# Two one-column VectorE operations of the softmaxes, with their further columns as per-partition scalars

## The chip, the cores and the metric

The kernel runs on one core of one Trainium2 chip. The metric is the time of one execution on the device, in microseconds (us). The core has a matrix engine (TensorE, PE in the rows; its weight loads are shown apart as PEld), three engines for elementwise work (VectorE or DVE, ScalarE or ACT, GpSimd or POOL), and SyncE (SP), which here only issues DMA transfers. Each engine takes its instructions in the order in which the program has them; semaphores hold an instruction until those it depends on are done.

## The reference

One decoder layer on 1024 tokens of 1024 features, in float32, in this order:

- a projection of the normalised input; its columns feed two groups of attention heads
- eight differential heads: `a = softmax(q1 k1 + bias) - lam * softmax(q2 k2 + bias)`, then `a @ v`, where `bias` falls with the distance of the positions and a causal mask is laid over both maps
- eight latent heads: `softmax(q k) @ v` with the causal mask
- the normalised heads through an output projection, added to the input
- attention to 256 memory tokens, and a mixture of 32 experts of which each token takes two; a last normalisation

The change lies in the two kinds of softmax over the 1024 tokens.

## The kernel before

All functions record instructions in a list; a planner (class `Sched`) with a small cost model starts them one after the other on a model of the engines, and the order in which it starts them is the order in the program. Its inputs are the recorded order, the dependences between the tiles, the room in the tile pools, and costs in nanoseconds: for VectorE `cost` (lines 232 to 238) charges 68 + 1.045 per element, with 60 more where an operand called `scalar` or standing third in an operation named `scalar...` is a tile, and 65 + 0.53 per element for a `tensor_scalar` in SBUF, with 60 more if any operand behind the first input is a tile. Nearly all instructions pass through one line, L481, so rows of the profile are told apart by the names of tiles.

The attention goes over items of one head and one half of the queries (512 of them, four blocks of 128). An item's softmaxes (`s_unit`) are recorded between the products with the values of the item before (`t_unit`, `f_unit`); other work (the memory's keys and values, parts of the output projection) is spread among them by a table of due times.

For a block of 128 queries, with one query per partition, the latent softmax (`softmax_mla`, L1020) multiplies queries and keys on TensorE into one or two banks of 512 keys, takes each bank's negated maximum on VectorE (`tensor_reduce`, L1032) into a column of the small tile `mx`, takes the smaller of the two columns where there are two banks (L1037, in 32 blocks: four of each of the eight heads), and lets ScalarE compute the exponentials with that column as bias and their sums (L1039). The bank comes free for TensorE after that.

The differential softmax (`softmax_diff`, L993) has two maps. For each, one VectorE instruction per bank adds the distance bias to the scores and keeps the minimum in a column of `mx` (L1006; CUSTOM_DVE_ANT_0 in the rows), and ScalarE makes the exponentials and their sums (L1011). Then VectorE takes the reciprocal of the second sum (L1013) and multiplies it with two further columns, `neglam` (minus lambda) and the first sum (L1014, in 64 blocks); with the product as a scalar per row GpSimd multiplies the second map and adds it to the first (L1015 and 1016; with FLEX = 4 the way on VectorE is not offered). These GpSimd operations read and write up to 1024 columns in SBUF. `mx` has seven buffers.

GpSimd also adds the two halves of a head's output (`O<-O,sh`), and makes some of the differences of split weights (`wlo`) and of `mix`. Further small chains on VectorE, `rs`, `g` and `fs`, are the norms' reciprocal roots, on 1 to 32 columns.

Of the kernel before, what the change touches and what calls it, by code (L numbers as in the profile page):

```python
# [17 lines left out]
OP = mybir.AluOpType  # L18
# [61 lines left out]
# Instructions are recorded with the tiles they read and write, and issued in the order in which  # L80
# a list scheduler with a simple cost model starts them.
# [6 lines left out]
def _sizes(side, kw, shape=None):  # L88
    """The axes of one side of a rearrange pattern, as lists of names."""
    out, group = [], None  # L90
    for tok in side.replace("(", " ( ").replace(")", " ) ").split():
        if tok == "(":
            group = []
        elif tok == ")":
            out.append(group)
            group = None
        elif group is None:
            out.append([tok])
        else:
            group.append(tok)  # L100
    return out


class View:
    """A part of a lazily allocated tile."""
# [58 lines left out]
class LazyTile:  # L164
    def __init__(self, pool, shape, dtype, kw, slot):
        self.pool, self.shape, self.dtype, self.kw, self.slot = pool, tuple(shape), dtype, kw, slot
        self.real, self.log, self.left, self.end = None, [], 0, 0
        self.seq, self.strict, self.reserve = slot["count"], False, slot["reserve"]
        self.cap = pool.sched.caps.get(kw["name"])
        slot["count"] += 1  # L170
        # a PSUM bank is taken only once all that is to be written there by the tensor engine can be
        self.whole, self.wait, self.at = pool.psum and kw["name"] != "acc", 0, 0
# [29 lines left out]
class Sched:  # L202
    def __init__(self, nc):
        self.nc, self.ops = nc, []
        self.free = dict.fromkeys(("tensor", "vector", "scalar", "gpsimd", "sync"), 0)
        self.dma_free, self.table = 0, 0
        # for tiles of some names, the places that they share
        self.caps = {n: [0] * c for n, c in dict(CAPS, bank=NB_S, acc=NB_A, lbank=NB_L).items()}
        self.window, self.busy, self.warm = 0, 0, False
        for e in self.free:  # L210
            setattr(self, e, Engine(self, e))
# [7 lines left out]
    def cost(eng, name, a, k, out, views):  # L219
        """Nanoseconds on the engine, and until the result is there."""  # L220
# [27 lines left out]
    def either(self, *ways):  # L248
        """Records an instruction, or a few of one engine; several ways: the scheduler chooses one."""
# [22 lines left out]
        for v in views:  # L272
# [3 lines left out]
            # the tensor engine's writes to a bank stay in order  # L276
# [3 lines left out]
            for o, b, ow in t.log:  # L280
                # the engines take turns at a bank, whatever they do there
                if o is not op and (t.pool.psum and (o.eng != eng or eng is None) or (w or ow) and (
                        fill and o.eng == "tensor" or all(x[0] < y[1] and y[0] < x[1] for x, y in zip(b, box)))):
                    op.deps.add(o)
# [8 lines left out]
    @staticmethod  # L293
    def hold(*views):
        """Instructions recorded after the next flush use these tiles too."""
        for v in views:
            v.tile.left += 1
# [6 lines left out]
    def flush(self):  # L304
# [17 lines left out]
        queue = {e: [] for e in self.free}     # (time ready, idx, op)  # L322
        avail = {e: [] for e in self.free}     # (idx, op)
# [6 lines left out]
        while done < len(ops):  # L330
            best = None
            for e in self.free:
# [4 lines left out]
                # the first one whose tiles have room  # L337
# [54 lines left out]
    @staticmethod  # L392
    def seen(op, eng):
        """When an engine can go on from an instruction."""
        if "dma" in op.name:
            return op.end
        if op.eng == eng == "tensor":
            return op.start
        return op.end + LAT[op.eng].get(eng, 170)

    def room(self, op):
        """When the tiles that the instruction is the first to use can be had; None: not known yet."""
# [16 lines left out]
        for slot, n, before, reserve in need.values():  # L419
            # some places are for the tiles that come before in program order  # L420
# [38 lines left out]
    def clock(self, now, cost):  # L459
        """The tensor engine's clock is halved after a window in which it was little busy."""  # L460
# [55 lines left out]
def hybrid_kernel(ctx: ExitStack, tc: tile.TileContext, a, out):  # L516
# [28 lines left out]
    # everything of size is a tile of 4 KB per partition  # L545
# [8 lines left out]
    def carve(name):  # L554
        """Small tensors as parts of such a tile."""
# [77 lines left out]
    def rsqrt(dst, v, tmp):  # L633
        """dst = 1 / sqrt(v): a first guess from the bits, and three steps of Newton's."""
# [7 lines left out]
    def rsqrt_mean(dst, ss, n, tmp):  # L642
        """dst = 1 / sqrt(ss / n + eps); ss is lost."""
# [3 lines left out]
    def two(name):  # L647
        """Two parts of a [128, 512] operand."""
        return t4(name, P, 2, CH, dt=F32R)
# [13 lines left out]
    def split(dst, src, g=None, eng="vector"):  # L663
        """src (times g) as the sum of two parts that the tensor engine takes exactly."""
# [7 lines left out]
    class Weights:  # L672
        """Column blocks of weights, loaded ahead of their use, in parts [rows, 128 of them, columns]."""
# [16 lines left out]
        def get(self, i):  # L690
            """A function from the row block to its two parts."""
# [12 lines left out]
    def weave(*lists):  # L704
        """Calls the units of all lists, each list's spread evenly over all or a part of the time."""
# [8 lines left out]
    # =================== projections ===================  # L714
# [26 lines left out]
    def x_first(t):  # L741
        """The same for one tile, so that the first products need not wait for a chunk."""
# [20 lines left out]
    # low-rank queries, keys and the rotary key, token-major  # L763
# [22 lines left out]
    # angles of the rotary part  # L786
# [4 lines left out]
    def reduce_angle(ang, tmp):  # L791
        """ang modulo 2 pi, within [-pi, pi] but for rounding"""
# [10 lines left out]
    def c_angles():  # L803
# [6 lines left out]
        # feature-major tables: even heads' has the rotary rows last, odd heads' first; the other rows scale only  # L810
# [32 lines left out]
    def out_split(po, dsts, g=None):  # L843
        """Two parts of a PSUM bank, stored; dsts: where to, and from which partitions."""
# [5 lines left out]
    # rotary key, four copies side by side  # L850
# [25 lines left out]
    # differential queries and keys  # L876
# [15 lines left out]
    # latent queries: columns of a head as [no position | rotary | rotary, halves swapped],  # L892
    # odd heads with the first part last
# [39 lines left out]
    def v_out(po, n0, nh, dst, t):  # L933
        """Values of nh heads from n0 on as [high | low] (even heads) and [low | high]."""
# [36 lines left out]
    # =================== attention ===================  # L971
# [12 lines left out]
    def make_dist(i):  # L984
        """-|pos_q - pos_k| / scale, and far below zero above the diagonal"""
# [7 lines left out]
    def softmax_diff(h, i, q, k, pt):  # L993
# [20 lines left out]
        nc.vector.scalar_tensor_tensor(mx[:, 4:5], mx[:, 3:4], neglam, sums[:, i, h:h + 1], op0=OP.mult, op1=OP.mult)  # L1014
# [5 lines left out]
    def softmax_mla(h, i, q, k, pt):  # L1020
# [14 lines left out]
        if len(scs) > 1:  # L1035
            top = mx[:, 2:3]
            nc.vector.tensor_tensor(top, mx[:, 0:1], mx[:, 1:2], op=OP.min)  # L1037
# [29 lines left out]
    def item(kind, h, c):  # L1067
        """Units of one head and half of its queries: the softmaxes, the products with the values."""
# [73 lines left out]
    def attention(items):  # L1142
        """All units of some items: an item's softmaxes along with the products of the one before."""
# [7 lines left out]
    # =================== output projection, memory, router ===================  # L1151
# [8 lines left out]
    # memory's keys and values  # L1160
# [47 lines left out]
    # output norms: one factor for each token and head  # L1208
# [70 lines left out]
    def factors(c, tiles, name):  # L1279
        """1 / rms of the rows of some tiles, in two steps."""  # L1280
# [10 lines left out]
    def cross_units(c):  # L1291
        """The rows of a chunk, transposed, times the gain and in two parts; their factors are for later."""
# [12 lines left out]
    # cross-attention  # L1305
# [78 lines left out]
    # router  # L1384
# [26 lines left out]
    def r_T(t, kk):  # L1411
        """Half a tile's columns, transposed and in two parts."""
# [19 lines left out]
    def r_keep(t):  # L1432
        """The tile's normalised rows, kept in DRAM for the experts."""
# [6 lines left out]
    def r_factors(c, *sizes):  # L1440
        """Units of the rows' factors, and of the tiles' transposes, logits and rows."""
# [16 lines left out]
    def first_max(v, m, oh, cm, wcol):  # L1458
        """One-hot of the first largest along the last axis, and the largest, step by step."""
# [16 lines left out]
    def r_top(c):  # L1476
        """The chunk's choices of experts."""
# [20 lines left out]
    def r_weights(c, take, gl, gm, goh, m12):  # L1498
# [15 lines left out]
        # in three exact parts  # L1514
# [13 lines left out]
    def r_rank(c):  # L1528
        """Rank of each choice among its expert's."""
# [25 lines left out]
    def r_index():  # L1555
        """The table of the first NS choices of every expert."""
# [15 lines left out]
    def r_slots():  # L1572
        """The weights of the table's choices."""
# [15 lines left out]
    def r_over():  # L1589
        """Blocks beyond an expert's first: how many, and where they start."""  # L1590
# [17 lines left out]
    # =================== experts ===================  # L1608
# [12 lines left out]
    def moe_piece(e, j):  # L1621
        """Of an expert's six pieces: two row blocks of gate and up each, or a row block of down."""
# [21 lines left out]
    def m_x(e):  # L1644
        """Gathers the expert's tokens and transposes them."""
# [81 lines left out]
    # =================== the order of it all ===================  # L1727
# [21 lines left out]
    # units of work on a common time line, which gives the priorities  # L1749
# [9 lines left out]
    def place(units, *knots):  # L1759
        """Spreads units over the stretches between knots, as many on each."""  # L1760
# [57 lines left out]
    # choices beyond an expert's first NS, in blocks of one expert each  # L1818
# [10 lines left out]
    with tc.If(rnov > 0):  # L1829
# [30 lines left out]
        # a choice that is among the first NS matches no lane  # L1860
# [88 lines left out]
    # =================== end: sum and norm ===================  # L1949
# [40 lines left out]
```

## Time and profile before

| | |
|---|---|
| runs | median 1263.01 us of 3 (1262.37 to 1264.27) |
| profiled execution | span 1263.7 us; no other time is given for it, so the span is taken as its own time |
| busy, share of the span | PE 89%, PEld 72%, DVE 72%, ACT 64%, POOL 33% |
| granted TensorE clock, mean | 0.928 |
| chain of waits | PE 49%, DMA 24%, DVE 15%, ACT 6% |

A busy share is the mean over stages. The first 180 us are projections, from 180 to 610 us the attention with other work in between, to 780 us the output projection and the memory attention, and from there to the end the router and the experts. The chain of waits is the work that ended last, followed from the last instruction back to what released it at each step.

### The profile page before, as it was taken

How to read it: one execution, taken by the hardware profiler on the slowest of the kernel's cores; microseconds unless marked ns; L12 is line 12 of the kernel's file. 1: busy time of each engine (PE TensorE's matmuls, PEld its weight loads, DVE VectorE, ACT ScalarE, POOL GpSimd, SP SyncE). 2: the span in 40 equal slices, each digit the busy share in tenths (PEclk: the TensorE clock that was granted, in tenths of full speed). 3: DMA queues.
4: the chain of work that ended last, by engine and by line, in shares of the span. 5: the costliest groups of instructions: out<-in, count | busy, mean ns of one | idle time of the engine just before them, and what ended most of it. 6: DMA issues, size and time to landing. Idle time of an engine off the chain costs nothing.

```text
span 1263.7 us, 19612 instructions
## 1 busy us (share of the span) xinstructions
PE 1119.0 (89%) x6285; PEld 915.9 (72%) x6285; DVE 903.8 (72%) x2100; ACT 803.1 (64%) x1597; POOL 423.3 (33%) x370
## 2 busy tenths in 40 slices
PE   4999999998888998888999999995999988888970
PEld 3988888896767876677899888874666656566640
DVE  5846525478799889988573467786678877777855
ACT  5744326679786778777371455632677877777862
POOL 2214311278554555746411001233133322221110
PEclk8999999997898999788999999995999999999995
DMA  9039897359636462445531132766899999999977
GB/s 291 18 106 314 316 356 223 110 169 265 155 96 146 123 162 62 114 121 194 173 122 47 34 103 70 284 233 232 251 293 275 299 291 311 307 316 315 334 218 272
DMA packets 177883, 256.56 MB, mean 203 GB/s; under 512 B 17035, under 2 KB 131058, under 8 KB 177778
## 3 DMA queue, kind: packets, MB, share of 16 engines
q1 hardware_dynamic: 161728, 208.22, 53.0%
q0 software_dynamic: 15680, 46.75, 12.2%
q8 instruction: 50, 0.82, 0.3%
q14 instruction: 55, 0.45, 0.1%
q10 hardware_dynamic: 370, 0.32, 0.1%
HBM read 208.57 MB, written 55.05 MB: 209 GB/s over the span
## 4 chain that ended last, share of the span: by engine, by line
PE 49%; DMA 24%; DVE 15%; ACT 6%; issue 4%; POOL 1%; SPq 0%; ACTq 0%; DVEq 0%; POOLq 0%
PE lbank L481 29%; DMA eraw<-in_w_expert_up_dram 16%; PE bank L481 15%; PE acc L481 5%; DMA eraw<-in_w_expert_down_dram 4%; DVE mx L481 4%; DVE pT L481 1%; ACT pt L481 1%; DVE pt L481 1%; DMA eraw<-in_w_expert_gate_dram 1%; DVE ss L481 1%; ACT pT L481 1%; DMA ACC<-y,gidx 1%; DVE yt L481 1%; DVE wlo L481 1%
## 5 line engine op out<-in xcount | busy, mean ns | idle before, releaser
L481 DVE TENSOR_TENSOR elo<-eraw,ehi 128x1024 fp32r<-128x1024 f32 x184 | 221.6, 1222 | 54.5 <-ACT ehi L481 50.7
L481 ACT CAST ehi<-eraw 128x1024 fp32r<-128x1024 f32 x184 | 189.6, 1050 | 38.8 <-DMA eraw<-in_w_expert_up_dram 28.5
L481 PE MATMUL bank<-ehi,xT 128*96 128x512 f32 x512 | 175.3, 414 | 16.8 <-ACT y L481 15.6
L481 PE MATMUL bank<-k,q 128*128 128x512 f32 (+5 forms) x480 | 137.6, 393 | 21.7 <-ACT pt L481 9.8
L481 DVE TENSOR_TENSOR pT<-bank,pT 128x512 fp32r<-128x512 f32 (+1 forms) x208 | 109.3, 560 | 31.6 <-ACT pT L481 31.2
L481 PEld LDWEIGHTS bank<-ehi,xT 128*96 128x96 f32 x512 | 86.4, 169 | 56.3 <-ACT y L481 19.3
L481 POOL DMA_INDIRECT ACC<-y,gidx x32 | 53.2, 1664 | 216.2 <-ACT y L481 150.3
L481 PE MATMUL acc<-pT,v 128*128 128x512 f32 (+3 forms) x384 | 116.3, 389 | 9.3 <-ACT pT L481 4.7
L481 PE MATMUL bank<-hc,pt 128*128 128x128 f32 x640 | 109.7, 301 | 8.8 <-POOL pt L481 3.2
L481 PEld LDWEIGHTS bank<-k,q 128*128 128x128 f32 (+1 forms) x480 | 87.1, 205 | 41.5 <-ACT pt L481 13.1
L481 ACT CAST pT<-bank 128x512 fp32r<-128x512 f32 (+1 forms) x208 | 93.2, 495 | 28.9 <-PE bank L481 27.7
L481 PE MATMUL bank<-elo,xT 128*96 128x512 f32 x256 | 105.3, 411 | 4.8 <-DVE elo L481 4.7
L481 PEld LDWEIGHTS bank<-hc,pt 128*128 128x128 f32 x640 | 86.6, 156 | 21.3 <-ACT pt L481 4.2
L481 PE MATMUL lbank<-whi,mix 128*128 128x256 f32 x512 | 96.6, 285 | 0.0
L481 PE MATMUL lbank<-whi,hT 128*128 128x256 f32 (+1 forms) x384 | 86.2, 312 | 0.0
L481 PEld LDWEIGHTS acc<-pT,v 128*128 128x128 f32 x384 | 67.5, 202 | 24.8 <-DVE pT L481 9.2
L481 PE MATMUL lbank<-hT,whi 128*128 128x512 f32 x256 | 81.6, 395 | 0.0
L481 PEld LDWEIGHTS lbank<-whi,mix 128*128 128x128 f32 x512 | 81.1, 191 | 0.1
L481 PE MATMUL bank<-ehi,hid 128*96 128x512 f32 x224 | 75.4, 395 | 1.8 <-DVE xT L481 1.0
L481 ACT ACTIVATE pt<-bank,mx 128x512 f32<-128x512 f32 (+2 forms) x96 | 55.3, 581 | 30.4 <-DVE mx L481 26.9
L481 DVE TENSOR_REDUCE mx<-bank 128x1 f32<-128x512 f32 (+3 forms) x112 | 61.2, 567 | 16.0 <-PE bank L481 15.8
L481 PE MATMUL lbank<-wlo,mix 128*128 128x256 f32 x256 | 72.4, 283 | 0.0
(622 smaller groups left out, 2703.9 us busy)
## 6 DMA issues: line engine op xcount, KB each, us to landing
eraw<-in_w_expert_gate_dram SPq DMA_DIRECT2D x128, 256.0 KB
eraw<-in_w_expert_up_dram SPq DMA_DIRECT2D x128, 256.0 KB
eraw<-in_w_expert_down_dram SPq DMA_DIRECT2D x64, 512.0 KB
k<-KD SPq DMA_DIRECT2D x72, 128.0 KB
QM<-st POOLq DMA_DIRECT2D x16, 512.0 KB, 5.3
q<-QM SPq DMA_DIRECT2D x16, 512.0 KB
wraw<-in_w_out_dram SPq DMA_DIRECT2D x16, 512.0 KB
wraw<-in_w_in_dram SPq DMA_DIRECT2D x12, 512.0 KB
```

Source lines behind the costliest of these rows:

```text
L481: getattr(getattr(self.nc, eng), name)(*[real(v) for v in a], **{n: real(v) for n, v in k.items()})
```

## The change

Two lines are written with another operation. Both operations are on one column (128 partitions of one element each), and the values computed are the same. In the first, `scalar_tensor_tensor` has two tensors as inputs, `mx[:, 3:4]` and `sums`, and `neglam` as a scalar per partition; the `tensor_scalar` has one tensor and two scalars per partition. In the second, `tensor_tensor` has two tensors, and the `tensor_scalar` one tensor and one scalar per partition. Elsewhere the change takes out comments and nothing else.

```diff
...
-        nc.vector.scalar_tensor_tensor(mx[:, 4:5], mx[:, 3:4], neglam, sums[:, i, h:h + 1], op0=OP.mult, op1=OP.mult)
+        nc.vector.tensor_scalar(mx[:, 4:5], mx[:, 3:4], neglam, sums[:, i, h:h + 1], op0=OP.mult, op1=OP.mult)
...
-            nc.vector.tensor_tensor(top, mx[:, 0:1], mx[:, 1:2], op=OP.min)
+            nc.vector.tensor_scalar(top, mx[:, 0:1], mx[:, 1:2], None, op0=OP.min)
...
```

By the cost model the first goes from 129 to 125.5 ns and the second from 69 to 125.5 ns, so the planner starts some instructions in another order. The first place where VectorE's rows stand otherwise is in the differential softmaxes of the first half of the queries (at about 304 us in the trace before). ISA is the score instruction of L1006 or, on one column, the read of its minimum; `p_` is the second map, with a running number. Before:

```order
L481 RECIPROCAL mx<-mx 128x1 x2
L481 ISA pt,mx<-bank,dist 128x512
L481 ISA mx 128x1
L481 SCALAR_TENSOR_TENSOR mx<-mx,lams,sums 128x1 x2
L481 ISA p__3426,mx<-bank,dist 128x512
L481 ISA mx 128x1
L481 RECIPROCAL mx<-mx 128x1
L481 SCALAR_TENSOR_TENSOR mx<-mx,lams,sums 128x1
```

VectorE at the same place now:

```order
L481 RECIPROCAL mx<-mx 128x1
L481 ISA pt,mx<-bank,dist 128x512
L481 ISA mx 128x1
L481 TENSOR_SCALAR mx<-mx,lams,sums 128x1
L481 RECIPROCAL mx<-mx 128x1
L481 ISA p__3421,mx<-bank,dist 128x512
L481 ISA mx 128x1
L481 TENSOR_SCALAR mx<-mx,lams,sums 128x1
L481 RECIPROCAL mx<-mx 128x1
L481 TENSOR_SCALAR mx<-mx,lams,sums 128x1
```

One reciprocal and its product stand behind the second map's score instead of ahead of it.

The second place is on VectorE in the second half of the queries, where the norms of four tokens' blocks (`rs`) run among the softmaxes (at about 412 us in the trace before). Before:

```order
L481 TENSOR_REDUCE mx<-bank 128x1
L481 TENSOR_REDUCE rs<-g_3855 128x4
L481 TENSOR_TENSOR mx<-mx 128x1
L481 TENSOR_SCALAR rs<-rs 128x4 x3
L481 TENSOR_TENSOR rs<-rs 128x4
L481 SCALAR_TENSOR_TENSOR rs<-rs 128x4
```

And now:

```order
L481 ISA p__4788,mx<-bank,dist,mx 128x512
L481 ISA mx 128x1
L481 TENSOR_REDUCE mx<-bank 128x1
L481 TENSOR_SCALAR rs<-rs 128x4
L481 TENSOR_SCALAR mx<-mx 128x1
L481 TENSOR_TENSOR rs<-rs 128x4
L481 SCALAR_TENSOR_TENSOR rs<-rs 128x4 x2
```

The three steps of `rs` that stood behind the minimum stand ahead of it, the last of them directly.

The third place is the issue of a differential head's loads on SP (at about 518 us in the trace before): `q` its queries, `k` its keys in two tiles of three transfers each, `v` its values. Before:

```order
L481 DMA k<-KP 64x2x512
L481 DMA v<-VM 128x8x128
L481 DMA q<-QD 32x2x512 x3
L481 DMA k<-KD 32x2x512 x6
L481 DMA v<-VD 128x8x128
```

And now:

```order
L481 DMA k<-KP 64x2x512
L481 DMA v<-VM 128x8x128
L481 DMA k<-KD 32x2x512 x3
L481 DMA q<-QD 32x2x512 x3
L481 DMA k<-KD 32x2x512 x3
L481 DMA v<-VD 128x8x128
```

The first tile of keys is loaded ahead of the queries; the rest stands as it stood.

## Rows read from the trace of the kernel before

**Rows 1.** The page: span, and busy time of the engines
```profile
span 1263.7 us, 19612 instructions
...
PE 1119.0 (89%) x6285; PEld 915.9 (72%) x6285; DVE 903.8 (72%) x2100; ACT 803.1 (64%) x1597; POOL 423.3 (33%) x370
```

**Rows 2.** Stretches: length, busy us of PE, PEld, DVE, ACT, POOL, clock, DMA, GB/s
```profile
325.00:610.00 285.00, 249.14 (x1448) 206.85 (x1446) 254.84 (x645) 218.50 (x487) 164.46 (x102) 0.90 0.46 125
...
610.00:780.00 170.00, 168.97 (x1173) 157.67 (x1174) 100.36 (x227) 82.46 (x164) 18.18 (x10) 0.99 0.29 95
780.00:1264.00 484.00, 399.91 (x1962) 287.26 (x1960) 351.18 (x608) 313.09 (x453) 121.98 (x85) 0.90 0.88 277
```

**Rows 3.** The chain of waits from 325 to 610 us, shares by tile
```profile
by line: PE bank L481 17.8%; DVE mx L481 16.4%; PE acc L481 8.8%; issue 8.6%; ACT pt L481 5.4%; DVE pt L481 4.8%; DVE pT L481 4.6%; PE lbank L481 3.1%; ACT pT L481 2.7%; DMA wraw<-in_w_mem_kv_dram 2.5%; POOL pt L481 2.0%; DVE g L481 1.9%; D
```

**Rows 4.** Groups, 178 to 610 us: count | busy us, mean ns | idle before
```profile
L481 DVE SCALAR_TENSOR_TENSOR mx<-mx,lams,sums 128x1 f32<-128x1 f32 x64 | 26.5, 417 | 0.6
...
L481 DVE TENSOR_TENSOR mx<-mx 128x1 f32<-128x1 f32 x32 | 17.9, 559 | 0.1
```

**Rows 5.** VectorE's instructions on mx: ns shortest/median/longest, first and last start
```profile
L481 DVE RECIPROCAL mx<-mx x72: 139/159/180, 257.8 to 779.2; 128x1 f32<-128x1 f32 x64, 128x4 f32<-128x4 f32 x8
L481 DVE SCALAR_TENSOR_TENSOR mx<-mx,lams,sums x64: 200/219/1915, 258.0 to 605.4; 128x1 f32<-128x1 f32 x64
L481 DVE TENSOR_TENSOR mx<-mx x32: 143/264/1469, 328.5 to 573.3; 128x1 f32<-128x1 f32 x32
L481 DVE CUSTOM_DVE_ANT_0 pt<-bank,dist,mx x32: 336/538/748, 357.2 to 600.0; 128x128 f32<-128x128 f32 x8, 128x256 f32<-128x256 f32 x8, 128x384 f32<-128x384 f32 x8, 128x512 f32<-128x512 f32 x8
...
L481 DVE TENSOR_SCALAR mx<-mx,fs x16: 198/222/228, 732.5 to 776.7; 128x2 f32<-128x2 f32 x16
```

**Rows 6.** Timeline, 415.5 to 419.5 us: start us, us, instruction [idle before]
```profile
416.13 1.89 POOL L481 TENSOR_TENSOR p__4785<-p__4785,mx 128x1024 f32<-128x1024 f32 x1 [1.57 <-DVE mx L481]
...
416.57 1.47 DVE L481 TENSOR_TENSOR mx<-mx 128x1 f32<-128x1 f32 x1
...
418.07 0.69 ACT L481 ACTIVATE pt<-bank,mx 128x512 f32<-128x512 f32 x1 [3.25 <-DVE mx L481]
...
418.10 2.37 POOL L481 TENSOR_TENSOR pt<-pt,p__4785 128x1024 f32<-128x1024 f32 x1
...
419.02 1.47 DVE L481 SCALAR_TENSOR_TENSOR rs<-rs 128x4 f32<-128x4 f32 x1
```

**Rows 7.** Timelines of VectorE and GpSimd, near 838 and 851 us
```profile
838.60 2.38 DVE L481 TENSOR_SCALAR fs<-fs 128x3 f32<-128x3 f32 x1 [0.50 <-ACT junk L481]
...
838.58 2.39 POOL L481 TENSOR_TENSOR xn<-xr,gb 128x1024 f32<-128x1024 f32 x1
...
851.55 0.34 DVE L481 TENSOR_SCALAR fs<-fs 128x1 f32<-128x1 f32 x2
...
850.56 3.29 POOL L481 TENSOR_TENSOR xn<-xr,gb 128x1024 f32<-128x1024 f32 x1 [9.60 <-DVE rper L481]
```

**Rows 8.** Tile ss: tensor_scalar with constants, nearly all on one column
```profile
L481 DVE TENSOR_SCALAR ss<-ss x39: 144/147/171, 11.2 to 1254.2; 128x1 int32<-128x1 int32 x24, 128x1 f32<-128x1 f32 x12, 128x4 int32<-128x4 int32 x2, 128x4 f32<-128x4 f32 x1
```

**Rows 9.** Pieces of the chain in order of time: start us, us, what
```profile
526.91 2.96 DMA k<-KD
...
565.38 5.34 DVE mx L481 x12
...
573.38 1.25 DVE mx L481 x2
```

**Rows 10.** Waits, 325 to 610 us: us in total, times, longest
```profile
ACT pt L481 <- DVE mx L481: 31.8, 27, 3.3
...
PEld bank L481 <- DVE mx L481: 11.6, 19, 3.2
```

**Rows 11.** Two stretches of 40 us, columns as in rows 2
```profile
300.00:340.00 40.00, 34.84 (x148) 28.22 (x147) 33.15 (x118) 32.40 (x96) 30.05 (x37) 0.65 0.71 172
340.00:380.00 40.00, 34.28 (x198) 26.70 (x196) 35.70 (x97) 35.46 (x87) 19.33 (x15) 1.00 0.47 121
```

## The prediction

> **What bounds the kernel now.** I read the views from the whole to the single instruction. First the page: the span is 1263.7 us and VectorE is busy for 72% of it [rows 1]. That mean is made of unlike stages, so next the windows [rows 2]. From 610 to 780 us TensorE is busy for 169 of 170 us: whatever comes before that stage in TensorE's order moves it. From 780 us on the DMA engines are busy for 88% of the time with the experts' weights, whose loads start when tiles of the earlier stages come free. The stage of the change, 325 to 610 us, has no engine that is full: TensorE 249 of 285 us, VectorE 255. The chain of waits says what sets its length [rows 3]: 16.4% of it, 46.7 us, is VectorE writing the small tile mx, the one-column values of the softmaxes. I take it that a microsecond saved between 325 and 610 us reaches the end, since the two stages behind are full from their first instruction on.
>
> Then the rows of mx itself [rows 4, 5]. A one-column instruction has one element per partition, so its time should hardly vary. The two-input minimum of the latent softmax goes from 143 to 1469 ns, the product of the differential softmax from 200 to 1915 ns, while the reciprocal of one column, which stands just ahead of that product, is never over 180 ns. The timeline shows what the long ones do [rows 6]: at 416.13 us GpSimd starts a product of 1.89 us; at 416.57 the minimum starts on VectorE and takes 1.47 us, to 418.04, 20 ns after GpSimd's end at 418.02. All 35 long ones (16 minima, 19 products) end so, beside the end of a GpSimd tensor operation. VectorE's queue is in order, so the reductions behind the minimum start only then, ScalarE's exponential waits for it (3.25 us idle in the same rows), and TensorE for the banks.
>
> **The change part by part.** *What goes.* 64 products, 26.5 us busy, would take 64 x 0.21 (between their shortest, 200, and their median, 219 ns) = 13.4 us without waits: 13.1 us of waiting. 32 minima, 17.9 us busy, would take 32 x 0.145 = 4.6 us: 13.3 us of waiting [rows 4, 5]. Together 26.4 us.
>
> *Do the new forms wait?* The trace has no one-column tensor_scalar with pointers beside GpSimd, but near ones [rows 5, 7]. A tensor_scalar on three columns waits: 2.38 us at 838.60, to the end of GpSimd's 2.39 us. Two on one column, inside a GpSimd operation that runs from 850.56 to 853.85, take 0.34 us together, no longer than elsewhere. The score instruction with a pointer, one tensor from SBUF and one from PSUM has a largest value of 748 ns in 32. So neither one column nor a pointer seems to make a wait; only several columns or a second SBUF tensor do. I take no wait at all for the new forms; the other end is the whole 26.4 us staying.
>
> The Trainium skill ("VectorE: DVE Perf Modes", What auto-detection actually checks) speaks against that: a single-source operation from SBUF to SBUF may enter a mode that uses both ports if the outermost non-unit sizes are even or equal. The three-column row agrees with it; the one-column rows wait for nothing, so by the rule read strictly the gain would be zero, and by the rows it is whole.
>
> *What is added.* A pointer costs something. One column with constants takes 147 ns [rows 8], two columns with a pointer 222 ns [rows 5]. For the minimum the bounds are 147 and 222 ns; I take 205, near the shortest product, which also reads one pointer: 32 x 0.06 = +1.9 us (0 to +2.4). For the product with two pointers the bounds are 200 ns and 222 + 75 = 297 ns; I take 222: 64 x 0.012 = +0.8 us (-0.6 to +5.6). VectorE's total falls by 26.4 - 2.7 = 23.7 us.
>
> *What of it is on the path.* Laid on the chain, the waiting between 325 and 610 us comes to 17.4 us, in 20 instructions; the longest and the last piece with some of it are in [rows 9]. The one of 5.34 us at 565.38 alone holds a minimum and a product with over 1 us of waiting each. 23 minima and 23 products lie on the chain at all, so the added cost there is 23 x 0.06 + 23 x 0.012 = 1.7 us. Net 15.7 us. Before 325 us GpSimd makes the products wait too, but the chain there has under 1 us of it, as TensorE's projections fill the time; I count that as nothing, and with the cover gone it would be that 1 us.
>
> *What is late next.* Not all of 15.7 us comes back. Direct waits of TensorE's weight loads for mx are 11.6 us, and ScalarE's exponentials wait 31.8 us for it [rows 10], some of it for ordinary work. And other small VectorE instructions keep two SBUF inputs: the one of rs at 419.02 us takes 1.47 us, waiting for the next GpSimd operation [rows 6]. Where the minimum is gone as the one that waits, the next such one meets GpSimd earlier. I take two thirds, 10.5 us; the ends are 0 and 15.7. On GpSimd itself little changes: it was running while the products waited, and its next product starts about 0.2 us sooner.
>
> *What is moved.* The planner's cost for the minimum rises from 69 to 125.5 ns and for the product falls from 129 to 125.5 ns, so it puts some instructions elsewhere. With the tiles' numbers left out, 176 of TensorE's 6435 rows, 108 of VectorE's 2211, 40 of ScalarE's 1315 and 4 of GpSimd's 390 stand elsewhere, nearly all in the attention; one subtraction of mix goes to GpSimd and one of wlo to VectorE. At the first place a product stands before the next score instead of behind it, a fraction of a microsecond early. At the second, one step of rs, on four columns, now stands ahead of the minimum, and can wait in its stead. At the third, SP issues half of a head's keys ahead of its queries; a load of these keys is 2.96 us of the chain at 526.91 [rows 9], so this may give or cost up to 3 us. I take 0 for the moves, with 3 us to either side.
>
> **Sum.** 1263.7 - 10.5 = 1253.2 us for the profiled execution; it stands 0.7 above the median of the timed runs, so 1252.5 us.
>
> **The rivals.** *The wait is passed on.* The operations of rs, g and mix that still read several columns or two tensors take over nearly all the waits. For it: the row at 419.02 and the new order at the second place. Against it: they are a few dozen, beside 96 changed ones. If nine tenths are passed on, 1.6 us stay: 1261.5.
>
> *The new order costs TensorE its clock.* This is the case on the other side. From 300 to 340 us the granted clock is 0.65, from 340 to 380 it is 1.00 [rows 11]; the mean of 0.90 over the 285 us [rows 2] means 57 us at 1.2 instead of 2.4 GHz, each time behind gaps in TensorE's work. If the moved rows leave TensorE without work at a new place, a stretch as from 300 to 340 costs half of 28 us, 14 us: 1252.5 + 14 = 1266.5. It decides from 21 us more at 1.2 GHz, where half of it eats the 10.5. Against it: TensorE's moved rows are few, and with shorter waits it should stand idle less.
>
> *The change doesn't take the wait away*, if a one-column tensor_scalar with pointers does wait for GpSimd. Then the 1.7 us on the path are all there is: 1263.0 + 1.7 = 1264.7. The one-column rows speak against it; that these have constants and not pointers leaves some room. The rule of the Trainium skill cited above ("VectorE: DVE Perf Modes") would lead here if a single column counts as equal sizes on both sides.
>
> **How the numbers follow.** The wait goes and most of it is won: 0.70, own range 1244 to 1259.5. Passed on: 0.11. The clock: 0.12. Still waits: 0.07. A run's difference of under 0.2%, 2.5 us, can't be told from none. Faster: 0.68 of the first and 0.03 of the second, 0.71; same: 0.02, 0.08 of the second, 0.05 of the last, 0.15; slower: 0.12 and 0.02, 0.14. The low end: 15.7 us won whole is 1247.3, and a fifth of the 57 us back at 2.4 GHz another 5.7, so 1241. The high end, 1266, takes in the passed-on waits, the pointer that still waits and nearly the case of the clock.
>
> **What would show it.** In the new profile the one-column tensor_scalar of mx should have largest values near their medians, about 205 and 222 ns, and busy times near 6.6 and 14.2 us; a largest value over 1 us would make the prediction wrong at its first step. VectorE's total should be near 880 us. The chain's share of mx between 325 us and the end of the attention should fall from 46.7 to some 30 us. If instead rs, g and mix show more long values, the wait was passed on; if the mean clock of the attention falls below 0.90, it is the third case. The stages behind should keep their lengths, 170 and 484 us, and only start sooner; if the last one grows by what the attention lost, my first assumption was wrong.

## The result, and the profile after

The changed kernel takes 1250.69 us (median of 4 runs, 1249.66 to 1254.27) beside 1263.64 us of the kernel before on the same chip: ratio 0.9892, 95% interval 0.9872 to 0.9911. It is faster by some 13 us, and the forecast of 1252.5 us is 1.8 us off. The profiled execution has a span of 1247.9 us and a mean granted clock of 0.936 (before 0.928).

The page, answering to [rows 1]:

```profile
span 1247.9 us, 19619 instructions
...
PE 1109.2 (89%) x6285; PEld 910.3 (73%) x6285; DVE 890.9 (71%) x2100; ACT 802.8 (64%) x1597; POOL 423.8 (34%) x370
```

VectorE is busy 12.9 us less, not the 23.7 us less of the forecast. The instructions on `mx` (shortest/median/longest in ns, first and last start) answer to [rows 5]:

```profile
L481 DVE RECIPROCAL mx<-mx x72: 138/162/178, 257.6 to 767.9; 128x1 f32<-128x1 f32 x64, 128x4 f32<-128x4 f32 x8
L481 DVE TENSOR_SCALAR mx<-mx,lams,sums x64: 256/269/275, 257.8 to 595.7; 128x1 f32<-128x1 f32 x64
L481 DVE TENSOR_SCALAR mx<-mx x32: 193/202/213, 327.6 to 565.8; 128x1 f32<-128x1 f32 x32
```

The spread is gone. The product takes 256 to 275 ns where it took 200 to 1915, the minimum 193 to 213 ns where it took 143 to 1469, though 39 of the 96 lie wholly inside a GpSimd tensor operation of this trace. The timeline of the stretch in [rows 6] (start us, length us, instruction, idle before it):

```profile
415.78 1.90 POOL L481 TENSOR_TENSOR p__4788<-p__4788,mx 128x1024 f32<-128x1024 f32 x1 [1.80 <-DVE mx L481]
...
416.22 0.20 DVE L481 TENSOR_SCALAR mx<-mx 128x1 f32<-128x1 f32 x1
...
416.45 0.69 ACT L481 ACTIVATE pt<-bank,mx 128x512 f32<-128x512 f32 x1 [2.08 <-DVE mx L481]
...
417.62 0.20 DVE L481 TENSOR_SCALAR mx<-mx 128x1 f32<-128x1 f32 x1
...
417.75 2.38 POOL L481 TENSOR_TENSOR pt<-pt,p__4788 128x1024 f32<-128x1024 f32 x1
...
417.93 2.23 DVE L481 SCALAR_TENSOR_TENSOR rs<-rs 128x4 f32<-128x4 f32 x1
```

GpSimd runs a product from 415.78 to 417.68 us. The minimum at 416.22 lies wholly inside it and takes 0.20 us; before, the one at the same place took 1.47 us, to GpSimd's end. ScalarE's exponential starts at 416.45, 0.03 us behind the minimum. The last row is the other side: a step of `rs` with two tensors on four columns takes 2.23 us, to 420.16, 0.03 us behind the end of GpSimd's addition (417.75 + 2.38). Before, such a step stood at 419.02 with 1.47 us; now one meets the addition earlier and waits longer.

Waits from 325 to 610 us, answering to [rows 10]: us in total, times, longest.

```profile
ACT pt L481 <- DVE mx L481: 19.9, 15, 4.5
...
PEld bank L481 <- DVE mx L481: 9.8, 15, 3.8
```

The exponentials wait 11.9 us less for `mx`, the weight loads 1.8 us less. The windows, answering to [rows 2] (busy us of PE, PEld, DVE, ACT, POOL, then clock, DMA share, GB/s):

```profile
325.00:610.00 285.00, 253.97 (x1504) 212.78 (x1503) 247.67 (x648) 221.18 (x491) 165.52 (x102) 0.92 0.49 134
610.00:780.00 170.00, 170.00 (x1161) 157.50 (x1161) 99.82 (x228) 81.23 (x162) 19.35 (x10) 1.00 0.27 85
780.00:1248.00 468.00, 387.98 (x1912) 278.99 (x1910) 347.95 (x600) 310.23 (x449) 119.51 (x84) 0.90 0.90 284
```

In the same 285 us there are 1504 matmuls where there were 1448, at a clock of 0.92 instead of 0.90. Not all of them are the attention's: its last product starts at 595.7 us instead of 605.4 [rows 5], so the window now ends with some 10 us more of the next stage. From 610 us on TensorE is full, as before. The chain of waits of this execution can't be followed through the attention; that of the same kernel profiled a second time (e6 below) can, and answers to [rows 3], 325 to 610 us:

```profile
by line: PE bank L481 22.3%; PE acc L481 9.6%; issue 8.2%; DVE mx L481 6.8%; DVE pT L481 6.7%; ACT pt L481 6.3%; DVE pt L481 3.6%; DVE wlo L481 3.1%; PE lbank L481 2.7%; DMA k<-KD 2.3%; ACT pT L481 2.0%; DMA k<-KP 1.8%; DVE rs L481 1.7%; DM
```

`mx` on VectorE has 6.8% of the 285 us, 19.4 us, where it had 46.7 and some 30 were forecast.

### The profile page after: what moved, and what is told of

Same layout as the page of the kernel before. It is cut to its first block, busy times and chain, and to the rows that moved or that the text cites. A ratio compares the mean times of both kernels' runs of the same rounds, so it can differ in the third digit from the quotient of the medians.

```text
span 1247.9 us, 19619 instructions
## 1 busy us (share of the span) xinstructions
PE 1109.2 (89%) x6285; PEld 910.3 (73%) x6285; DVE 890.9 (71%) x2100; ACT 802.8 (64%) x1597; POOL 423.8 (34%) x370
## 5 line engine op out<-in xcount | busy, mean ns | idle before, releaser
L481 PE MATMUL bank<-ehi,xT 128*96 128x512 f32 x512 | 178.7, 422 | 19.1 <-ACT y L481 18.3
L481 PE MATMUL bank<-k,q 128*128 128x512 f32 (+5 forms) x480 | 131.4, 381 | 19.4 <-ACT pt L481 7.8
L481 DVE TENSOR_TENSOR pT<-bank,pT 128x512 fp32r<-128x512 f32 (+2 forms) x208 | 109.6, 560 | 29.7 <-ACT pT L481 28.9
L481 ACT CAST pT<-bank 128x512 fp32r<-128x512 f32 (+2 forms) x208 | 93.4, 494 | 33.9 <-PE bank L481 33.0
L481 PEld LDWEIGHTS bank<-k,q 128*128 128x128 f32 (+1 forms) x480 | 84.1, 198 | 37.0 <-DVE mx L481 11.5
L481 PEld LDWEIGHTS acc<-pT,v 128*128 128x128 f32 x384 | 66.1, 197 | 25.7 <-DVE pT L481 11.3
L481 DVE TENSOR_REDUCE mx<-bank 128x1 f32<-128x512 f32 (+3 forms) x112 | 61.3, 567 | 15.7 <-PE bank L481 15.5
```

The source lines that it names most:

```text
L481: getattr(getattr(self.nc, eng), name)(*[real(v) for v in a], **{n: real(v) for n, v in k.items()})
```

## The experiments

The theory: an instruction on VectorE with two tensors in SBUF, or with several columns, waits for the end of a GpSimd operation that is running, and one with one column and one tensor does not; the gain is that waiting, as far as it lies on the chain. Rivals: the new order makes the gain; the number of tensors alone counts, whatever the columns; the waiting is worth the same wherever it stands. The planner's costs can be set apart from the operations, so operations and order are tried one by one. Ratios are to the kernel before on the same chip, with medians of 1264.61 us (e1 to e4), 1265.63 (e5 to e8) and 1265.05 (e9 to e12).

| | operations | order | median us | ratio, interval |
|---|---|---|---|---|
| e1 | both new | old | 1245.74 | 0.9841 (0.9819 to 0.9863) |
| e2 | both old | the change's | 1266.08 | 1.0007 (0.9992 to 1.0022) |
| e3 | minimum new | old | 1251.64 | 0.9887 (0.9865 to 0.9908) |
| e4 | product new | old | 1255.70 | 0.9922 (0.9904 to 0.9940) |
| e5 | as e1, minimum on two columns | old | 1259.19 | 0.9939 (0.9916 to 0.9962) |
| e6 | the change again | the change's | 1252.16 | 0.9896 (0.9871 to 0.9921) |
| e7 | both new in the last items only | old | 1249.63 | 0.9871 (0.9847 to 0.9895) |
| e8 | both new in all others | old | 1262.44 | 0.9980 (0.9965 to 0.9995) |
| e9 | both new | product charged as before | 1250.98 | 0.9891 (0.9866 to 0.9916) |
| e10 | both new | minimum charged as before | 1248.08 | 0.9872 (0.9850 to 0.9894) |
| e11 | both new | charged as measured | 1248.29 | 0.9870 (0.9851 to 0.9890) |
| e12 | e1 again | old | 1245.55 | 0.9849 (0.9827 to 0.9871) |

**e1, operations without order.** The planner is charged what the old operations cost, so every engine's instructions stand as before.

```diff
         if eng == "vector":
+            if out.tile.kw["name"] == "mx" and name == "tensor_scalar" and isinstance(a[2], View):
+                if isinstance(a[3], View):
+                    return 68 + 60 + 1.045, 0, 0
+                if a[2].tile is out.tile:
+                    return 68 + 1.045, 0, 0
```

> Both new instructions, but the planner is charged the old costs (129 and 69 ns), so every engine's order is that of the kernel before. Theory (the waits for GpSimd were on the path and are gone): nearly all of the gain, 11 to 15 us against before, 1249 to 1253 us; minimum and product never over 280 ns. Rival (the planner's new order brought the gain): within 3 us of before, 1261 to 1264 us.

0.9841: the operations alone give 20 us, more than the whole change, and more than the 11 to 15 expected.

**e2, order without operations.** The same hook turned round: the old operations are charged 125.5 ns.

> Both old instructions, but the planner is charged the new cost (125.5 ns for each), so every engine's order is that of the changed kernel. Theory: within 4 us of before, 1260 to 1268 us, and some 26 us of waiting again in the minimum and the product. Rival (the order): 1249 to 1254 us.

1.0007: with the old operations the order is worth nothing. The gain is the operations'; that the order takes some of it back shows only beside them.

**e3 and e4, one operation each**, in the old order.

> Only the minimum is new, in the old order. Theory, by the waiting on the chain of the kernel before (12.7 us in minima, 4.7 us in products): the larger part, 8 to 11 us of gain, 1253 to 1256 us. Rival (each microsecond off VectorE's queue counts alike, and minima and products waited 13 us each): half the gain, 6 to 7 us, 1257 us.

VectorE's instructions on `mx` in e3 (shortest/median/longest ns):

```profile
L486 DVE SCALAR_TENSOR_TENSOR mx<-mx,lams,sums x64: 202/219/2375, 258.0 to 596.2; 128x1 f32<-128x1 f32 x64
L486 DVE TENSOR_SCALAR mx<-mx x32: 189/204/215, 328.8 to 566.4; 128x1 f32<-128x1 f32 x32
```

> Only the product is new, in the old order. Theory, by the chain: 4.7 us of waiting on it less 23 x 0.055 us of dearer products (269 against 213 ns), so 2 to 4 us of gain, 1260 to 1262 us. Rival (each microsecond off VectorE's queue counts alike): 5 to 7 us of gain, 1257 us; if the dearer product eats it, none.

The same in e4:

```profile
L486 DVE TENSOR_SCALAR mx<-mx,lams,sums x64: 257/269/276, 258.4 to 598.2; 128x1 f32<-128x1 f32 x64
L486 DVE TENSOR_TENSOR mx<-mx x32: 147/498/1735, 328.3 to 565.7; 128x1 f32<-128x1 f32 x32
```

In each, the operation that is left in the old form keeps its long ones (to 2375 and 1735 ns) and the other is flat. Their gains are 14.3 and 9.9 us. Both lie above what the waiting on the chain gave for them (8 to 11 and 2 to 4 us), the product's above its rival's 5 to 7 too, so the chain's shares don't price them. They add up to 24.2 us where both together win 20; with 2 to 3 us to either side of each, that isn't clearly more than the sum.

**e5, two columns.** The minimum in its new form on two columns, of which the second isn't used:

```diff
-            nc.vector.tensor_scalar(top, mx[:, 0:1], mx[:, 1:2], None, op0=OP.min)
+            nc.vector.tensor_scalar(mx[:, 2:4], mx[:, 0:2], mx[:, 1:2], None, op0=OP.min)
```

> As e1 (both new instructions, old order), but the minimum is taken of two columns at once: out mx[:, 2:4], in mx[:, 0:2], still one pointer and no second tensor; the further column is not used. Theory (what keeps an instruction from waiting for GpSimd is that it has a single column and a single tensor): the minima wait again, with largest values over 1 us and some 13 us or more in all, and the time is that of e4_product_only, 7 to 11 us under before, 1253 to 1257 us. Rival (the second tensor input is all that counts): largest value under 250 ns, and the time of e1, 17 to 20 us under before, 1244 to 1248 us.

The same in e5:

```profile
L486 DVE TENSOR_SCALAR mx<-mx,lams,sums x64: 255/268/274, 258.9 to 603.0; 128x1 f32<-128x1 f32 x64
L486 DVE TENSOR_SCALAR mx<-mx x32: 211/508/1745, 330.0 to 570.4; 128x2 f32<-128x2 f32 x32
```

One tensor and a pointer, but two columns: it waits again, up to 1745 ns, and the gain falls to 6.4 us, a little under the 7 to 11 expected and, within the intervals, that of the product alone (0.9939 beside 0.9922 in e4). So dropping the second tensor isn't enough by itself; this `tensor_scalar` must also be on one column.

That several columns make an instruction wait doesn't hold for every operation. In the trace of the kernel before (start us, length us, instruction):

```profile
404.50 3.38 POOL L481 TENSOR_TENSOR wlo<-wraw,whi 128x1024 fp32r<-128x1024 f32 x1
...
406.42 0.34 DVE L481 RECIPROCAL g<-sums 128x32 f32<-128x32 f32 x1
...
406.79 1.15 DVE L481 TENSOR_TENSOR g<-ssq,g 128x32 f32<-128x32 f32 x1
```

The reciprocal has one tensor of 32 columns, runs inside a GpSimd operation that ends at 407.88 us, and takes 0.34 us, as it does elsewhere (336 and 353 ns in its two instances). The operation with two tensors behind it takes 1.15 us, to 407.94. So what is shown for several columns is shown for `tensor_scalar`.

**e6, the change again**, beside e5, e7 and e8.

> The changed kernel once more, beside the same runs of before as the other kernels of this call. Theory (the planner's new order costs 5 to 6 us where the waits are gone): ratio to before 0.988 to 0.991, 12 to 15 us of gain, against 19 us of e1 in the old order. Rival (e1 and the first runs of the changed kernel differ by the occasion): ratio 0.983 to 0.986, 18 to 21 us of gain.

0.9896 beside 0.9892: the change's own time holds.

**e7 and e8, where the waiting is worth something.** e7 has the new operations only in the last items, from about 495 us on; e8 only in those before.

```diff
-        nc.vector.tensor_scalar(mx[:, 4:5], mx[:, 3:4], neglam, sums[:, i, h:h + 1], op0=OP.mult, op1=OP.mult)
+        if i >= TPC and h in (1, 5, 6, 7):
+            nc.vector.tensor_scalar(mx[:, 4:5], mx[:, 3:4], neglam, sums[:, i, h:h + 1], op0=OP.mult, op1=OP.mult)
+        else:
+            nc.vector.scalar_tensor_tensor(mx[:, 4:5], mx[:, 3:4], neglam, sums[:, i, h:h + 1], op0=OP.mult, op1=OP.mult)
...
-            nc.vector.tensor_scalar(top, mx[:, 0:1], mx[:, 1:2], None, op0=OP.min)
+            if h >= 6:
+                nc.vector.tensor_scalar(top, mx[:, 0:1], mx[:, 1:2], None, op0=OP.min)
+            else:
+                nc.vector.tensor_tensor(top, mx[:, 0:1], mx[:, 1:2], op=OP.min)
```

> Old order; new instructions only where they run after about 500 us: the minima of heads 6 and 7, and the products of heads 1, 5, 6 and 7 in the second half of the queries (8 minima, 16 products; 7.7 of the 26.3 us of waiting of before). Theory (until about 500 us something else sets the pace, and the gain comes behind it, with TensorE's clock): most of e1's gain, 12 to 17 us, 1248 to 1253 us. Rival (each waiting on the chain counts alike, 6.0 of 17.4 us): 6 to 7 us, 1258 us.

> Old order; new instructions in all places but those of e7_late_only (24 minima, 48 products; 18.6 of the 26.3 us of waiting). Theory: 0 to 5 us of gain, 1260 to 1265 us. Rival (each waiting on the chain counts alike): 12 us, 1252 us.

I summed the waiting in the traces: for each VectorE instruction that ends within 60 ns behind a GpSimd operation, what it takes beyond its usual length. Of 26.3 us that products and minima lose to it, e7 takes away 7.7 and wins 16.3 us; e8 takes away 18.6 and wins 2.5. The windows from 500 us to the start of each kernel's last product (columns as above), so that nearly the same work lies in each; first the kernel before:

```profile
500.00:605.40 105.40, 91.65 (x491) 75.72 (x489) 96.61 (x237) 80.98 (x171) 68.00 (x38) 0.82 0.45 133
```

e8:

```profile
500.00:605.00 105.00, 91.46 (x485) 75.51 (x483) 95.54 (x236) 80.10 (x168) 66.96 (x38) 0.82 0.46 133
```

e7:

```profile
500.00:588.90 88.90, 82.70 (x485) 67.21 (x485) 85.44 (x235) 79.35 (x170) 67.55 (x38) 0.94 0.56 157
```

The change:

```profile
500.00:595.70 95.70, 87.25 (x481) 71.96 (x481) 87.91 (x233) 80.04 (x168) 67.01 (x37) 0.88 0.51 146
```

e8 repeats the kernel before, at the same clock, and is 0.4 us shorter. e7 is 16.5 us shorter, and the rows say where: TensorE is busy 82.70 us instead of 91.65, 9.0 less, and idle 6.2 us instead of 13.8, 7.6 less. A clock of 0.82 means that 38 of the 105 us are at 1.2 GHz, 0.94 that 11 of the 89 are. So nearly half of the gain is idle time of TensorE that goes with the waits, and up to half is nearly the same matmuls (485 beside 491) taking less time at the higher clock.

Ahead of 500 us the windows differ little (a clock of 0.95 before and 0.94 in e8, from 325 to 500 us), and what is won there is not there any more at 500: VectorE's instructions in e8 are at most 2.5 us ahead of those before, and 1.0 us at 500, while the loads of this stretch are issued at most 1.0 us earlier. That e8's early gain is lost to loads, and that half of the late gain goes through the clock, is read from these traces; no run took the loads' or the clock's share away by itself.

**e9 to e12, what the order costs.** The new operations throughout; the planner is charged 125.5 ns for the minimum and 129 for the product (e9), 69 and 125.5 (e10), 204 and 269 as measured (e11), 69 and 129 (e12, as e1). Beside e1, e11 reads:

```diff
                 if isinstance(a[3], View):
-                    return 68 + 60 + 1.045, 0, 0
+                    return 269, 0, 0
                 if a[2].tile is out.tile:
-                    return 68 + 1.045, 0, 0
+                    return 204, 0, 0
```

> New operations as in the change; the planner is charged 125.5 ns for the minimum (as in the change) and 129 ns for the product (as before). Its order holds the swap of keys and queries at the third place, and one more such swap at the next latent head. Theory A (the swap of the loads in the last heads is what the order costs): as the change or worse, ratio 0.989 to 0.993. Theory B (each order is a draw, none of its moves by itself decides): anywhere from 0.984 to 0.995.

> New operations as in the change; the planner is charged 69 ns for the minimum (as before) and 125.5 ns for the product (as in the change). The keys stand ahead of the queries one differential head earlier than at the third place, which itself stands as before. Theory A (the swap at the third place costs the 6 us): about 0.985, as with the old order. Theory B (a draw): anywhere from 0.984 to 0.995.

> New operations as in the change; the planner is charged what they were measured to take, 204 ns for the minimum and 269 ns for the product. Some 780 rows stand elsewhere than before, more than twice as many as in the change; the third place stands as before. Theory A (the swap at the third place costs): about 0.985. Theory B (a draw): anywhere from 0.984 to 0.995; truer costs give no better order than the old ones. A third theory, that the planner does better with true costs: under 0.984.

> The new operations in the old order once more, beside these three: 0.984 (0.982 to 0.986), if the first measurement holds.

Five orders, one set of operations: 0.9849 and 0.9841 (old), 0.9870, 0.9872, 0.9891, and 0.9892 and 0.9896 (the change's). The three with the keys issued ahead of the queries at the third place (the change twice, and e9) give 0.989 to 0.990, the others 0.984 to 0.987. The change's order is clearly above the old one (0.9894 against 0.9845 in the mean, 6 us of 1265). e10 and e11 lie some 3 us above the old order, about as much as the intervals allow, and e9 isn't clear of them. True costs give no better order than the old ones.

What the change's order loses is sought first in the chain of e6, start us, length us, what:

```profile
551.44 0.45 PE bank L481 x4
551.89 0.17 SPq L481
...
552.57 0.42 SPq L481
...
553.10 4.56 DMA v<-VD
557.66 0.07 DVE mx L481
```

TensorE's work is followed by SP issuing the last differential head's loads, the values last, at 553.10, and by their 4.56 us, before VectorE goes on at 557.66. SP's own rows say when they come, first in e6 (start us, us in the queue, which load):

```profile
522.77 1.31 SPq L481 DMA_DIRECT2D q<-QD  x3
...
548.90 1.27 SPq L481 DMA_DIRECT2D q<-QD  x3
...
553.10 0.38 SPq L481 DMA_DIRECT2D v<-VD  x1
```

And in e12, in the old order:

```profile
517.06 1.27 SPq L486 DMA_DIRECT2D q<-QD  x3
...
542.86 1.27 SPq L486 DMA_DIRECT2D q<-QD  x3
...
547.11 0.38 SPq L486 DMA_DIRECT2D v<-VD  x1
```

The chain of e12 has no load at this place. The chain of e2, the same order as e6 with the old operations, has this load of the values too (4.47 us, at 558.99); none of the chains of the kernels in the old order has it (those of e11 and of the change's first profile can't be followed). But the load isn't the 6 us. When the last head's queries are issued, e6 is already 6.0 us behind e12 (548.90 beside 542.86), and so it is when the values are issued (553.10 beside 547.11); at the last product it is 6.8 us behind (596.6 beside 589.8). So the load has at most some 1 us of it, and the rest is lost ahead of it. The first rows show a lag ahead of it: at the third place, behind the first keys, the queries are issued 5.7 us later (522.77 beside 517.06), though the next head's come at 531.0 us in e6 and 531.2 in e12. In the change and e9 they come at 521.8 and 522.2 us, in e10 and e11 at 517.1 and 519.1. That fits the swap as the cause, but it isn't shown: no run has the swap alone, and in e2 the swap is there (queries at 526.16 us, beside 518.31 before) and costs nothing with the old operations.

## Why the prediction was right, and where it was off

**The waits go: right.** 35 long instructions were counted, none is left in 96. The step "neither one column nor a pointer seems to make a wait" held in every run. Its other half, "only several columns or a second SBUF tensor do", e5 bore out for `tensor_scalar`; for a reciprocal several columns make no wait, as its row of 32 columns above shows. The rule cited from the Trainium skill ("VectorE: DVE Perf Modes", What auto-detection actually checks) asks whether the outermost non-unit sizes are even or equal. The two columns of e5 agree with it, if entering that mode is what waits, which no run shows by itself. A single column has no such size, so the rule doesn't speak of it: "read strictly the gain would be zero" took a size of one as equal, and the 96 that don't wait put that reading out.

**What is added: the minimum right, the product undersized.** The minimum takes 202 ns at the median (205 forecast). The product takes 269 and not 222: I took one pointer's price for two. Constants alone take 147 ns [rows 8], one pointer 202, two 269, so each adds 55 to 67. 64 x 0.047 = 3.0 us more on VectorE. Of the other miss in VectorE's total, 23.7 less forecast and 12.9 found, 5.3 us are waiting that other instructions took over: the sum over all VectorE instructions fell from 46.2 to 25.2, by 21.0 and not 26.3. The `rs` of 2.23 us above is such a piece. One more `wlo` on VectorE, moved by the planner, has 1.3 us. Some 1 us stays open.

**What of it comes back: the mechanism right, "two thirds" wrong.** In the old order 1.55% or 19.6 us (the mean of e1 and e12) come back, more than the 15.7 us on the chain. Two things were missing. The waiting ahead of 500 us is worth almost nothing (e8), so the chain's 17.4 us were not one currency. And that behind 500 us is worth twice itself (e7), since TensorE's idle time goes and its clock in that stretch rises from 0.82 to 0.94. My range took "a fifth of the 57 us back at 2.4 GHz" as its low end only; here some 24 of 38 us came back between 500 us and the last product in e12, whose row is:

```profile
500.00:589.80 89.80, 84.07 (x486) 68.86 (x486) 85.67 (x235) 79.41 (x170) 67.67 (x38) 0.92 0.54 156
```

**The moves: 0 with 3 us to either side was too narrow.** They take 6 us. The place was named (the loads at about 518 us), and a lag of e6 shows there, though not as a load of the keys on the chain: the queries behind them come 5.7 us later. That the swap makes the 6 us isn't shown. The two wrong sizes, 9 us too little for the waits and 6 us too little for the moves, nearly cancel: a good part of the 1.8 us of error is luck.

**The rivals.** Passed on: true for 5 of 26 us. The new order costs TensorE its clock: not against the kernel before (0.92 to 0.90), but against its own operations in the old order it does, 0.88 beside 0.92 in the windows above; there TensorE is busy 3.2 us longer (87.25 and 84.07) and idle 2.7 us longer (8.4 and 5.7). Still waits: no.

**The stages behind keep their lengths: nearly.** The reciprocals of four columns, in the stage that TensorE fills, end with one at 779.2 us before [rows 5] and 767.9 after, 11.3 us sooner; the span ends 15.8 us sooner. The 4 us beyond are no gift of the attention, since e8 has them too, with a span of 1259.6 us and its last such reciprocal at 778.9: from there to the end it is 480.7 us. Before it is 484.5 us, the longest of all profiles; in the other thirteen it lies between 479.6 and 483.8, whatever waits they have (480.4 in e2, with all of them). The row of e8:

```profile
L486 DVE RECIPROCAL mx<-mx x72: 135/160/180, 257.8 to 778.9; 128x1 f32<-128x1 f32 x64, 128x4 f32<-128x4 f32 x8
```

## What to carry to other kernels

Where small VectorE instructions have a spread of ten to one and the long ones end with a GpSimd operation, look for a form with one tensor input and one column, and give further columns as scalars: it costs some 60 ns a pointer, and here two such lines, run 96 times, were worth 20 us. Price such a wait by the stage: ahead of 500 us, at a clock of 0.95, it was worth a seventh of itself; behind, where the gaps in TensorE's work go with a clock of 0.82, twice itself. And keep the order of the program apart from the operation when a planner's cost changes with it: the best kernel measured is the new operations in the old order, 1245.7 and 1245.6 us, some 6 us below the change as it was made.

## What the runs showed of the hardware that I had not expected

- A `tensor_scalar` with one pointer on one column takes 202 ns and with two 269, beside 147 with constants; the pair of pointers costs no less than twice one.
- Two columns are enough to make a `tensor_scalar` wait: the same instruction on one column is never over 215 ns in 32, on two it is up to 1745 ns (e5). A reciprocal of 32 columns doesn't wait (0.34 us inside a GpSimd operation, before).
- A wait that is taken away is partly found again on the next instruction with two tensors or, for a `tensor_scalar`, several columns: 5.3 of 26.3 us.
- Some 8 us of waiting on VectorE that go (e7) shorten the same stretch of TensorE's work by 16.5 us, from 105.4 to 88.9: 7.6 us less idle and 9.0 us less busy, with the granted clock rising from 0.82 to 0.94.
